# The prompt joins the projections' first pass over the sample, raw tokens are split, and the norm's root is multiplied in at the evacuations

## The chip, the cores and the metric

The kernel runs on one core of a Trainium2 chip. The metric is the device time of one execution in microseconds (us), as the median of several runs. The engines are PE (TensorE: matmuls; PEld its weight loads), DVE (VectorE), ACT (ScalarE), POOL (GpSimd) and SP (SyncE, which issues nearly all transfers). Each works through its own queue in order, and they wait for one another at semaphores.

## What is computed

One encoder layer is applied to a prompt of 256 tokens and a sample of 2048 tokens, with the same weights. The part that matters here is the first:

```python
h = rms_norm(x, norm_mix_g)
proj = h @ w_in
q, k, v, x_br, y_br = jnp.split(proj, splits, axis=-1)
q = rms_norm(q.reshape(B, S, N_Q_HEADS, HEAD_DIM), q_norm_g)
k = rms_norm(k.reshape(B, S, N_KV_HEADS, HEAD_DIM), k_norm_g)
...
attn = bidir_gqa(apply_axial_rope(q, tables), apply_axial_rope(k, tables), v)
rec = recurrent_group(x_br, y_br, conv_w, conv_b, lru_wa, lru_ba, lru_wx, lru_bx, lru_lambda)
x = x + jnp.concatenate([attn, rec], axis=-1) @ w_out
```

`rms_norm` divides a token by the root of its mean square, so the root is one number per token and could be taken before or after `h @ w_in`. `w_in` has 1024 rows and 1792 columns. The recurrent group runs a convolution, two gates and a forward and a backward scan on `x_br`, and multiplies by the gelu of `y_br`. After this come the output projection, an MLP and a last norm.

## The kernel before

All arrays lie feature-major (128 features on the partitions, tokens along the row). Every large matmul is done as three: weights and activations are each split into a rounded high part and a low remainder, and `mm3` adds high x high, high x low and low x high. `w_in` is cut into 14 blocks `m` of 128 output columns: 0 to 3 are the queries, 4 the keys, 5 the values, 6 to 9 the four recurrent channels, 10 to 13 the gelu's. `project` multiplies one block with one tile of tokens: 24 matmuls, 256 tokens wide for the prompt and 512 for each of the four sample tiles. Its sum stands in one of three PSUM banks (`m0` to `m2`, two while the prompt's attention holds `m2`), and `evac` moves it to SBUF.

The first stage makes three passes over the 14 blocks. The prompt's pass (`order_p`) loads each weight tile, rounds it (line 168), subtracts (line 177) and stores both parts; two passes over the sample follow, `ORDER_S` for tiles 0 and 1 and `ORDER_T` for tiles 2 and 3, which read the stored parts back. `WStream.advance` keeps these streams some tiles ahead.

`norm1` squares a tile of tokens, sums over features (a matmul with ones), takes the reciprocal root with a Newton step and multiplies the tokens by it; `norm1_split` then makes the parts `hh` and `hl` with the norm's gain. The pool of these parts holds two sets, so tiles 2 and 3 enter when the last block of tiles 0 and 1 has been multiplied.

Around the projections run generators, advanced by `tick` twice in each `project`: `do_gelu`, `do_qk` (head norm and rotary embedding), `do_v`, `lru` for one recurrent channel at a time, and `attention_p`, the prompt's attention for a pair of head blocks, started at block 1 of each sample pass and waited for before block 9 of the first and block 12 of the second. A scheduler with a timeline of its own sets the final order on each engine; `evac` has a raised priority. When the 28 sample block pairs are done, the second stage begins: the prompt's output projection and MLP, the backward scans (`lru_back`) and the sample's attention, interleaved, and then the four MLPs of the sample.

## Time and profile before

| | |
|---|---|
| median of 3 runs | 3201.34 us (3199.52 to 3202.33) |
| the profiled execution | 3204.86 us |
| its span, first to last instruction | 3203.1 us |
| busy share of the span: PE, DVE, ACT, POOL | 94%, 57%, 54%, 45% |
| mean granted TensorE clock | 0.966 of full speed |

Busy shares are means over stages that differ: PE is busy nearly throughout the long MLP and attention stages, and much less in the first quarter of the span. A matmul counts as busy from its start to a modelled end, and matmuls overlap, so the step from one start to the next is the better measure of what one costs.

### The profile page before, as it was taken

How to read it: one execution, taken by the hardware profiler on the slowest of the kernel's cores; microseconds unless marked ns; L12 is line 12 of the kernel's file. 1: busy time of each engine (PE TensorE's matmuls, PEld its weight loads, DVE VectorE, ACT ScalarE, POOL GpSimd, SP SyncE). 2: the span in 40 equal slices, each digit the busy share in tenths (PEclk: the TensorE clock that was granted, in tenths of full speed). 3: DMA queues.
4: the chain of work that ended last, by engine and by line, in shares of the span. 5: the costliest groups of instructions: out<-in, count | busy, mean ns of one | idle time of the engine just before them, and what ended most of it. 6: DMA issues, size and time to landing. Idle time of an engine off the chain costs nothing.

```text
span 3203.1 us, 41975 instructions
## 1 busy us (share of the span) xinstructions
PE 3009.3 (94%) x13646; PEld 2431.3 (76%) x13646; DVE 1823.7 (57%) x2602; ACT 1720.3 (54%) x2988; POOL 1438.2 (45%) x1117
## 2 busy tenths in 40 slices
PE   6699899678999899999999999999999999899998
PEld 5577677566888588888887888888878888778887
DVE  8878776699787754555556555555573311121114
ACT  5465666455666566555556655555566333343333
POOL 4436633577888654334356434433654201411104
PEclk7799999788999899999999999999999999999999
DMA  7656455888766554444456544444664655766554
GB/s 255 200 177 225 158 182 187 257 270 248 236 219 208 170 190 130 148 137 130 148 170 226 166 141 137 139 142 134 218 208 154 189 189 188 261 230 188 188 189 148
DMA packets 346044, 598.98 MB, mean 187 GB/s; under 512 B 44128, under 2 KB 77152, under 8 KB 345824
## 3 DMA queue, kind: packets, MB, share of 16 engines
q1 hardware_dynamic: 345824, 596.30, 58.0%
q8 instruction: 107, 1.75, 0.2%
q14 instruction: 113, 0.93, 0.1%
HBM read 474.52 MB, written 121.63 MB: 186 GB/s over the span
## 4 chain that ended last, share of the span: by engine, by line
PE 68%; DVE 7%; DMA 5%; ACT 3%; issue 2%; POOL 1%; SPq 1%; DVEq 0%; ACTq 0%; POOLq 0%
PE ps_d L204 8%; PE ps_d L202 8%; PE ps_d L203 8%; PE ps_u L204 8%; PE ps_u L203 8%; PE ps_u L202 8%; PE s_t L974 3%; PE s_t L975 3%; PE pq L980 3%; PE po L979 3%; PE s_mx L870 3%; PE ps_o L203 1%; PE ps_o L202 1%; PE ps_o L204 1%; DVE mx L871 1%
## 5 line engine op out<-in xcount | busy, mean ns | idle before, releaser
L990 POOL TENSOR_TENSOR acc<-acc,ph 128x512 f32<-128x512 f32 x448 | 598.8, 1337 | 534.1 <-ACT ph L984 521.6
L168 ACT CAST wh<-wf 128x512 fp32r<-128x512 f32 x712 | 440.2, 619 | 720.7 <-PE ps_d L203 296.2
L986 DVE TENSOR_TENSOR pl<-s_t,ph 128x512 fp32r<-128x512 f32 x512 | 349.6, 684 | 278.6 <-ACT ph L984 274.6
L204 PE MATMUL ps_u<-h2h,wl 128*128 128x512 f32 (+1 forms) x1280 | 479.4, 375 | 7.2 <-DMA wl<-wl_d 3.7
L202 PE MATMUL ps_u<-h2h,wh 128*128 128x512 f32 (+1 forms) x1280 | 478.4, 374 | 0.8 <-DVE xr L1013 0.8
L203 PE MATMUL ps_u<-h2l,wh 128*128 128x512 f32 (+1 forms) x1280 | 478.9, 374 | 0.0
L982 ACT ACTIVATE s_t<-s_t 128x512 f32<-128x512 f32 x512 | 298.1, 583 | 327.5 <-PE s_t L975 310.7
L202 PE MATMUL ps_d<-uh,wh 128*128 128x512 f32 (+1 forms) x1248 | 466.1, 373 | 2.1 <-ACT rl L1031 0.8
L204 PE MATMUL ps_d<-uh,wl 128*128 128x512 f32 (+1 forms) x1248 | 465.8, 373 | 2.2 <-DVE wl L177 1.3
L203 PE MATMUL ps_d<-ul,wh 128*128 128x512 f32 (+1 forms) x1248 | 465.3, 373 | 0.3 <-DVE ul L1035 0.2
L871 DVE TENSOR_REDUCE mx<-s_mx 128x1 f32<-128x512 f32 x512 | 344.1, 683 | 210.5 <-PE s_mx L870 208.8
L1033 POOL TENSOR_TENSOR rl<-rl 128x512 f32<-128x512 f32 (+1 forms) x160 | 159.2, 995 | 626.9 <-ACT uh L1032 620.5
L1146 DVE TENSOR_TENSOR y<-y,ps_d 128x512 f32<-128x512 f32 (+1 forms) x272 | 170.5, 627 | 323.3 <-PE ps_d L204 321.0
L984 ACT ACTIVATE ph<-s_t 128x512 fp32r<-128x512 f32 x512 | 304.7, 597 | 27.7 <-POOL acc L990 2.0
L1035 DVE TENSOR_TENSOR ul<-rl,uh 128x512 fp32r<-128x512 f32 (+1 forms) x160 | 145.9, 912 | 289.3 <-POOL rl L1033 289.2
L204 PEld LDWEIGHTS ps_u<-h2h,wl 128*128 128x128 f32 x1280 | 243.4, 190 | 57.4 <-DMA wl<-wl_d 5.0
L202 PEld LDWEIGHTS ps_u<-h2h,wh 128*128 128x128 f32 x1280 | 243.4, 190 | 50.9 <-DVE xr L1013 1.4
L203 PEld LDWEIGHTS ps_u<-h2l,wh 128*128 128x128 f32 x1280 | 243.3, 190 | 48.3 <-issue 0.5
L202 PEld LDWEIGHTS ps_d<-uh,wh 128*128 128x128 f32 x1248 | 236.4, 189 | 53.0 <-ACT rl L1031 2.2
L204 PEld LDWEIGHTS ps_d<-uh,wl 128*128 128x128 f32 x1248 | 236.1, 189 | 50.1 <-DVE wl L177 2.3
L203 PEld LDWEIGHTS ps_d<-ul,wh 128*128 128x128 f32 x1248 | 236.3, 189 | 48.0 <-DVE ul L1035 1.2
L202 PE MATMUL ps_in<-hh,wh 128*128 128x512 f32 (+1 forms) x560 | 220.8, 396 | 44.1 <-DVE wh L168 16.4
(281 smaller groups left out, 5704.2 us busy)
## 6 DMA issues: line engine op xcount, KB each, us to landing
wl<-wl_d SPq DMA_DIRECT2D x624, 256.0 KB, 2.7
wf<-in_w_up_dram SPq DMA_DIRECT2D x320, 256.0 KB, 3.0
wf<-in_w_down_dram SPq DMA_DIRECT2D x320, 256.0 KB, 3.0
wl_d<-wl SPq DMA_DIRECT2D x172, 256.0 KB, 3.0
wf<-in_w_out_dram SPq DMA_DIRECT2D x80, 256.0 KB, 4.0
wh<-wh_d SPq DMA_DIRECT2D x56, 256.0 KB, 3.4
x<-in_xT_dram SPq DMA_DIRECT2D x32, 256.0 KB, 4.8
qd<-q_ds SPq DMA_DIRECT2D x64, 128.0 KB, 3.0
```

Source lines behind the costliest of these rows:

```text
L168: self.copy(i)(tile_, self.f[i])
L202: mm(ps, wh, xh, start=first, stop=False)
L203: mm(ps, wh, xl, start=False, stop=False)
L204: mm(ps, wl, xh, start=False, stop=last)
L871: nc.vector.tensor_reduce(mx[:, i, b:b + 1], s[:, :w], axis=AX.X, op=ALU.max)
L982: act(s, s, AF.Exp)
L984: act(ph, s, AF.Copy)
L986: tt(pl, s, f32(ph), op=ALU.subtract)
L990: gtt(acc, acc, f32(ph), op=ALU.add)
L1033: gtt(e[:, :n], e[:, :n], e[:, :n], op=ALU.mult)
L1035: tt(ul[:, f, :n], e[:, :n], f32(uh[:, f, :n]), op=ALU.subtract)
L1146: tt(y[:, :n], y[:, :n], ps[:, :n], op=ALU.add)
```

## The change

There is no prompt pass any more. In the pass over tiles 0 and 1, each weight block is multiplied first with the prompt's 256 tokens, then with the two sample tiles; weights are loaded, split and stored in this pass and read back once, in the pass over tiles 2 and 3. The tokens are split into parts without the norm's root (`split`); the sum of squares and the root are made beside it (`squares`, `roots`), and `evac` multiplies by the root on DVE, where ACT copied before. The rounding of the weights goes to ACT after the first six tiles. In `do_gelu` a multiply leaves POOL and a scale-and-add leaves DVE for one DVE operation; in `do_qk` a square moves from POOL to ACT and a multiply from DVE to POOL. The split gate weights of a channel are stored at first use and read back later, where they were rebuilt each time. The prompt's attention runs wholly in the second pass. Both orders of blocks are new.

```diff
-NORM_AT = 9
+RAW_AT = 13
-ORDER_S = [6, 0, 2, 7, 13, 12, 8, 4, 1, 3, 11, 5, 9, 10]
-ORDER_T = [4, 5, 0, 6, 1, 10, 8, 2, 11, 7, 3, 12, 9, 13]
+ORDER_S = [0, 6, 1, 10, 7, 2, 11, 8, 3, 12, 9, 13, 4, 5]
+ORDER_T = [6, 4, 5, 7, 0, 1, 8, 2, 3, 9, 10, 11, 12, 13]
-PA_AT = [1, 1]
+PA_AT = 2
 PA_END = 12
...
-    def evac(dst, src):
+    def evac(dst, src, r):
+
         with tc.high_priority(offset=EVAC):
-            act(dst, src, AF.Copy)
+            tt(dst, src, r, op=ALU.mult)
...
-    ws = WStream(wp, srcs, saved, AHEAD, WBUFS, lambda i: nc.vector.tensor_copy if i < n1 else nc.scalar.copy,
+    ws = WStream(wp, srcs, saved, AHEAD, WBUFS, lambda i: nc.vector.tensor_copy if i < 6 else nc.scalar.copy,
...
+        g_d = [[dtile([P, 512], f"g{t}_d{c}") for t in "hl"] for c in range(4)]
+        gate_split = set()
+
 
         def load_gates(c):
+            if c in gate_split:
+                parts = [cp.tile([P, 2, 2, P], FR, tag=t, name=t, bufs=2) for t in ("wgh", "wgl")]
+                for t, d in zip(parts, g_d[c]):
+                    loadr(t.rearrange("p g d n -> p (g d n)"), d)
+                return parts
+            gate_split.add(c)
...
+            for t, d in zip((wgh, wgl), g_d[c]):
+                store(d, f32(t).rearrange("p g d n -> p (g d n)"))
...
-        def do_gelu(dst, n, ps):
+        def do_gelu(dst, n, ps, r):
             y = sl.tile([P, NT], F32, tag="gy", name="gy", bufs=2)
             z = sl.tile([P, NT], F32, tag="gz", name="gz", bufs=2)
-            evac(y[:, :n], ps[:, :n])
-            act(z[:, :n], y[:, :n], AF.Square)
-            ts(z[:, :n], z[:, :n], 0.044715, 1.0, op0=ALU.mult, op1=ALU.add)
-            yield
-            gtt(z[:, :n], z[:, :n], y[:, :n], op=ALU.mult)
+            evac(y[:, :n], ps[:, :n], r)
+            act(z[:, :n], y[:, :n], AF.Square, scale=math.sqrt(0.044715))
+            yield
+            stt(out=z[:, :n], in0=z[:, :n], scalar=1.0, in1=y[:, :n], op0=ALU.add, op1=ALU.mult)
             yield
...
-                gtt(t[:, :w], rr, rr, op=ALU.mult)
+                act(t[:, :w], rr, AF.Square)
...
-                tt(qq, qq, rr, op=ALU.mult)
+                gtt(qq, qq, rr, op=ALU.mult)
...
+        def enter(xs, t):
+
+            while not sets:
+                yield
+            sets.pop(0)
+            h = h_tiles()
+            yield from split(xs, *h)
+            h_s.append(h)
+            acc = yield from squares(xs, NT)
+            r = r_tile()
+            yield from roots(acc, NT, r)
+            r_s.append(r)
...
         for hf in range(2):
+            tiles = [("s", 2 * hf, NT * 2 * hf), ("s", 2 * hf + 1, NT * (2 * hf + 1))]
+            if hf == 0:
+                tiles = [("p", None, 0)] + tiles
             for ii, m in enumerate((order_s, order_t)[hf]):
-                i = len(order_p) + hf * len(order_s) + ii
+                i = hf * len(order_s) + ii
+                end = ii == len(order_s) - 1
                 ws.advance(2 * i)
-                if hf == 0 and ii == NORM_AT:
-                    while pa in ticks.active:
+                if hf == 0 and ii == RAW_AT:
+                    while convs.get(0, 1) or any(g in ticks.active for g in qk_p):
                         tick()
-                    banks[0] = itertools.cycle(("m0", "m1", "m2"))
-                    nxt = [load_x(SEQ + NT * t, NT, tag) for t, tag in ((2, "xb"), (3, "xa"))]
-                    spawn(norms(nxt))
-                if ii == PA_AT[hf]:
+                    entering.append((load_x(SEQ + 2 * NT, NT, x_tiles("xb")), 2))
+                if hf == 1 and ii == PA_AT:
                     banks[0] = itertools.cycle(("m0", "m1"))
-                    pa = spawn(attention_p([2 * hf]))
-                if hf and ii == PA_END:
+                    pa = spawn(attention_p([0, 2]))
+                if hf == 1 and ii == PA_END:
                     while pa in ticks.active:
                         tick()
                     banks[0] = itertools.cycle(("m0", "m1", "m2"))
...
+                for r, t, t0 in tiles:
+                    if t is None:
+                        ps = project(i, h_p, SEQ)
+                        root = r_p
+                        if 6 <= m < 10:
+                            x = xp.tile([P, NT], F32, tag="xb", name="xb_p")
+                            xb_p.append(x)
+                            nc.vector.memset(x[:, 0:2], 0.0)
...
+                        if end:
+                            entering.append((load_x(SEQ + 3 * NT, NT, x_tiles("xa")), 3))
+                        continue
+                    while len(h_s) <= t:
                         tick()
-                    ps = project(i, h_s[2 * hf + t], NT)
-                    if ii == len(order_s) - 1:
+                    ps = project(i, h_s[t], NT)
+                    if end:
                         sets.append(t)
+                    while len(r_s) <= t:
+                        tick()
+                    root = r_s[t]
+                    o = NT * (t % 2)
                     if 6 <= m < 10:
-                        evac(xb[:, off + NT * t:off + NT * t + NT], ps)
+                        evac(xb[:, off + o:off + o + NT], ps, root)
                     elif m >= 10:
-                        spawn(do_gelu(gel_d["s"][m - 10, :, t0:t0 + NT], NT, ps))
+                        spawn(do_gelu(gel_d["s"][m - 10, :, t0:t0 + NT], NT, ps, root))
```

The new functions (`split` and `squares` yield now and then, so that other work comes between):

```python
def split(xs, hh, hl):

    for k in range(KC):
        act(hh[k], xs[k], AF.Identity, scale=vcol(V_GMIX + k))
        stt(out=hl[k], in0=xs[k], scalar=vcol(V_GMIX + k), in1=f32(hh[k]), op0=ALU.mult, op1=ALU.subtract)
        if k % 2:
            yield

def squares(xs, n):
    acc = sb.tile([P, NT], F32, tag="acc", name="acc")
    for k in range(KC):
        if k == 0:
            act(acc[:, :n], xs[k], AF.Square)
        else:
            s = sb.tile([P, NT], F32, tag="b", name="sq", bufs=3)
            act(s[:, :n], xs[k], AF.Square)
            gtt(acc[:, :n], acc[:, :n], s[:, :n], op=ALU.add)
        if k % 2:
            yield
    return acc

def roots(acc, n, r):
    ps = ps_a.tile([P, 2, NT], F32, tag="st", name="ps_n")
    mm(ps[:, 0, :n], ones_d, acc[:, :n], start=True, stop=True)
    yield
    w = sb.tile([P, NT], F32, tag="b", name="w1", bufs=3)
    rsqrt_newton(ps[:, 0, :n], r, w[:, :n], tt)
    ts(r, r, -0.5, None, op0=ALU.mult)
    yield
...
def start():
    yield from split(xs_p, *h_p)
    ws.advance(0)
    acc = yield from squares(xs_p, SEQ)
    h = h_tiles()
    yield from split(xs0, *h)
    h_s.append(h)
    yield from roots(acc, SEQ, r_p)
    h = h_tiles()
    yield from split(xs1, *h)
    h_s.append(h)
    for xs in (xs0, xs1):
        acc = yield from squares(xs, NT)
        r_s.append(r_tile())
        yield from roots(acc, NT, r_s[-1])
```

At the start of the program, on PE: before, the prompt's blocks follow one another (`hh` and `hl` are the prompt's parts, each `wh`/`wl` number a weight tile, 256 wide).

```order
L203 MATMUL ps_in<-hl,wh_507 128x256
L204 MATMUL ps_in<-hh,wl_516 128x256
L202 MATMUL ps_in<-hh,wh_507 128x256
L203 MATMUL ps_in<-hl,wh_507 128x256
L204 MATMUL ps_in<-hh,wl_516 128x256
L202 MATMUL ps_in<-hh,wh_564 128x256
L203 MATMUL ps_in<-hl,wh_564 128x256
L204 MATMUL ps_in<-hh,wl_570 128x256
```

After, at the same place (`hp` are the prompt's parts, `hh` and `hl` now a sample tile's, 512 wide):

```order
L205 MATMUL ps_in<-hp,wl_431 128x256
L203 MATMUL ps_in<-hp,wh_422 128x256
L204 MATMUL ps_in<-hp,wh_422 128x256
L205 MATMUL ps_in<-hp,wl_431 128x256
L204 MATMUL ps_in<-hl,wh_419 128x512
L205 MATMUL ps_in<-hh,wl_428 128x512
L203 MATMUL ps_in<-hh,wh_419 128x512
L204 MATMUL ps_in<-hl,wh_419 128x512
```

A weight tile, split once (`wh_419`), now serves three token tiles in a row where it served the prompt alone.

On DVE in the first part of the program: before, in the prompt's pass, the rounding (`CAST`) and the subtraction of weight tiles stand in nearly every row.

```order
L168 CAST wh_903<-wf_896 128x512
L177 TENSOR_TENSOR wl_909<-wf_896,wh_903 128x512
L411 TENSOR_TENSOR wgl<-wgf,wgh 128x512
L168 CAST wh_1008<-wf_898 128x512
L177 TENSOR_TENSOR wl_1014<-wf_898,wh_1008 128x512
L429 TENSOR_SCALAR gz<-gz 128x256
L403 MEMSET wgf 128x512
```

After, the evacuations (line 197) of the first two blocks, behind the root (`r_527` is that of sample tile 0, `r_559` of tile 1):

```order
L324 TENSOR_SCALAR r_527<-r_527 128x512
L197 TENSOR_TENSOR qk<-ps_in,r_527 128x512
L197 TENSOR_TENSOR xb<-ps_in,r_527 128x512
L529 SCALAR_TENSOR_TENSOR xc<-xb,vec,xc 128x512 x2
L210 TENSOR_TENSOR w_562<-r_559 128x512
L211 SCALAR_TENSOR_TENSOR w_562<-ps_n,w_562 128x512
L212 SCALAR_TENSOR_TENSOR r_559<-w_562,r_559 128x512
L324 TENSOR_SCALAR r_559<-r_559 128x512
L197 TENSOR_TENSOR qk<-ps_in,r_559 128x512
```

The evacuations came onto DVE, and the first of each tile stands behind that tile's root.

At the end of the first stage, on PE: before, the last channel's gate matmuls (`ps_g`) follow the first twelve matmuls of the prompt's output projection (`ps_o`), which follow the last projection.

```order
L204 MATMUL ps_o<-cat_4915,wl_5249 128x256
L202 MATMUL ps_o<-cat_4915,wh_5245 128x256
L203 MATMUL ps_o<-cat_4917,wh_5245 128x256
L204 MATMUL ps_o<-cat_4915,wl_5249 128x256
L202 MATMUL ps_g<-xh,wgh 128x342
L203 MATMUL ps_g<-xl,wgh 128x342
L204 MATMUL ps_g<-xh,wgl 128x342
```

After, the prompt's attention (`pdenp`, its last matmuls) stands just ahead of the last 24 matmuls of the projections, and no gate matmul stands behind them:

```order
L205 MATMUL ps_in<-hh,wl_4917 128x512
L689 MATMUL pdenp<-ahp,ones_312 128x512
L689 MATMUL pdenp<-alp,ones_312 128x512
L689 MATMUL pdenp<-ahp,ones_315 128x512
L689 MATMUL pdenp<-alp,ones_315 128x512
L203 MATMUL ps_in<-hh,wh_4818 128x512
```

The recurrent tail moved ahead of the last blocks, and the end of the prompt's attention moved behind most of them.

## Rows read from the trace of the kernel before

**Rows 1.** Busy time by stretch: window, length, PE, PEld, DVE, ACT, POOL, clock, DMA, GB/s.

```profile
0.00:127.00 127.00, 77.28 (x404) 68.19 (x404) 108.14 (x183) 59.46 (x118) 62.41 (x50) 0.74 0.69 231
127.00:353.00 226.00, 205.07 (x843) 157.38 (x844) 178.70 (x226) 138.09 (x209) 111.06 (x72) 0.97 0.61 201
353.00:579.00 226.00, 204.43 (x872) 161.52 (x872) 161.54 (x202) 146.72 (x220) 99.07 (x63) 0.95 0.51 170
579.00:640.00 61.00, 38.96 (x185) 31.36 (x184) 39.48 (x50) 30.46 (x50) 30.45 (x22) 0.75 0.98 297
640.00:800.00 160.00, 128.16 (x644) 103.36 (x643) 149.11 (x187) 88.63 (x175) 119.70 (x91) 0.86 0.86 260
```

**Rows 2.** Timeline of ACT: the last evacuation of each pass; start, length.

```profile
126.92 0.38 ACT L196 ACTIVATE v<-ps_in 128x256 f32<-128x256 f32 x1 [2.75 <-PE ps_in L204]
...
352.16 0.58 ACT L196 ACTIVATE gy<-ps_in 128x512 f32<-128x512 f32 x1
...
578.88 0.60 ACT L196 ACTIVATE gy<-ps_in 128x512 f32<-128x512 f32 x1
```

**Rows 3.** Timeline of PE: first and last of 46 projection matmuls in a row.

```profile
310.03 0.39 PE L204 MATMUL ps_in<-hh,wl 128*128 128x512 f32 x1
...
320.26 0.39 PE L204 MATMUL ps_in<-hh,wl 128*128 128x512 f32 x1
```

**Rows 4.** Waits of PE, 0 to 127 us: total, times, longest.

```profile
PE ps_in L202 <- DVE wh L168: 16.4, 5, 6.4
PE ps_in L204 <- DVE wl L177: 13.0, 10, 3.6
```

**Rows 5.** Groups of DVE by shape, 0 to 579 us: count, busy, mean ns, idle before.

```profile
L331 DVE SCALAR_TENSOR_TENSOR hl<-x,vec,hh 128x512 fp32r<-128x512 f32 x32 | 29.9, 977 | 6.7 <-ACT hh L330 6.7
...
L177 DVE TENSOR_TENSOR wl<-wf,wh 128x512 fp32r<-128x512 f32 x29 | 24.7, 853 | 1.2
...
L478 DVE TENSOR_TENSOR ql<-qk,qh 128x512 fp32r<-128x512 f32 x20 | 22.6, 1132 | 5.2 <-ACT qh L476 5.0
L168 DVE CAST wh<-wf 128x512 fp32r<-128x512 f32 x28 | 21.4, 766 | 4.3 <-DMA wf<-in_w_in_dram 4.2
...
L429 DVE TENSOR_SCALAR gz<-gz 128x512 f32<-128x512 f32 x15 | 17.5, 1165 | 2.3 <-ACT gz L428 2.3
L471 DVE TENSOR_TENSOR qk<-qk,rq 128x512 f32<-128x512 f32 x20 | 16.7, 852 | 0.7 <-POOL qk L464 0.5
...
L468 DVE SCALAR_TENSOR_TENSOR wq<-ps_q,wq 128x512 f32<-128x512 f32 x22 | 14.8, 682 | 5.6 <-POOL wq L467 5.6
...
L411 DVE TENSOR_TENSOR wgl<-wgf,wgh 128x512 fp32r<-128x512 f32 x12 | 13.7, 1145 | 4.1 <-ACT wgh L409 4.1
...
L435 DVE SCALAR_TENSOR_TENSOR gz<-gz,gy 128x512 f32<-128x512 f32 x15 | 12.0, 798 | 11.6 <-ACT gz L433 11.6
...
L669 DVE RECIPROCAL rcp<-pdenp 128x512 f32<-128x512 f32 x2 | 6.7, 3358 | 0.1
...
L662 DVE TENSOR_TENSOR alp<-pfp,ahp 128x512 fp32r<-128x512 f32 x4 | 5.6, 1407 | 3.2 <-ACT ahp L661 3.2
L649 DVE TENSOR_TENSOR plp<-pfp,php 128x512 fp32r<-128x512 f32 x8 | 5.5, 683 | 0.5 <-ACT php L647 0.5
L631 DVE TENSOR_REDUCE mxp<-s_mxp 128x2 f32<-128x512 f32 x8 | 5.5, 683 | 3.4 <-PE s_mxp L629 3.4
```

**Rows 6.** Groups of POOL by shape, 0 to 579 us, same columns.

```profile
L315 POOL TENSOR_TENSOR x<-x,r 128x512 f32<-128x512 f32 x32 | 49.9, 1592 | 5.6 <-DVE r L310 5.6
...
L431 POOL TENSOR_TENSOR gz<-gz,gy 128x512 f32<-128x512 f32 x15 | 24.0, 1598 | 18.5 <-DVE gz L429 18.5
```

**Rows 7.** Waits of PE, 127 to 579 us: the longest in total.

```profile
PE ps_in L202 <- ACT qk L196: 10.5, 2, 5.6
```

**Rows 8.** Timelines of PE and DVE: first sample-attention matmul, last forward scan.

```profile
598.48 1.19 PE L870 MATMUL s_mx<-k,qd 128*128 128x512 f32 x2 [5.64 <-DMA qd<-q_ds]
...
605.81 4.08 DVE L560 TENSOR_TENSOR_SCAN s<-af,cfw,s 128x1026 f32<-128x1026 f32 x1
```

More of the change, by code (lines that the diff above doesn't have):

```diff
@@ L565, in lru_prompt @@
             done = []
[L566 removed]
+            gate_w.clear()
+            yield from lru([(xb[c], SEQ * c, SEQ, c) for c in range(4)],
                            [(SEQ * c, SEQ, c, None) for c in range(4)], 4 * SEQ, done, 0)
@@ L731, in trunk, with enter_all @@
-        sets.append(0)
+        def enter(xs, t):
+            while not sets:
+                yield
+            sets.pop(0)
[6 more added lines that the diff above has]
+            r_s.append(r)
+        entering = []
+        def enter_all():
+            while len(h_s) < 4:
+                while not entering:
+                    yield
+                xs, t = entering.pop(0)
+                yield from enter(xs, t)
```

201 lines of the change are left out of this document (82 added, 119 removed).

## The prediction

> **What bounds the kernel now.** I read the busy times by stretch first [rows 1], cut where the last evacuation of each pass over the projections stands [rows 2]: the prompt's pass ends at 127 us, the first half of the sample at 353 us, the second at 579 us. The reader should compare PE with DVE in each line. In the prompt's pass PE is busy 77 of 127 us and DVE 108, or 85%. PE's granted clock there is 0.74, between its two levels of 1.2 and 2.4 GHz, against 0.97 in the next stretch. In each half of the sample PE is busy 205 of 226 us and DVE only 179 and 162. From 579 to 640 us nobody is full (PE 39 and DVE 39.5 of 61), and from 640 to 800 us DVE is busy 149 of 160, or 93%. Behind 800 us the change does nothing; whatever it is worth must come from the first 640 us.
>
> The step of a sample matmul is (320.26 - 310.03)/45 = 0.227 us [rows 3]. The prompt's 336 matmuls have half the columns, so I estimate half the step, 0.114 us, and 38 us in all. The prompt's pass takes 127 us for 38 us of matmuls, because weights are prepared for a matmul that uses them only briefly: PE's longest waits in it are for the rounding of the weights (16.4 us) and for their subtraction (13.0 us), both on DVE [rows 4]. So the prompt's pass is bound by DVE and the sample's passes mostly by PE, with DVE having room beside it. The change lays the first two stretches over each other.
>
> **The merged pass.** Its PE work is that of the first half, 205 us busy, and 38 us of the prompt: 243 us. Its DVE work starts from 108.1 + 178.7 = 286.8 us [rows 1]. The durations below are in [rows 5]; a form 256 wide is put at half of the form 512 wide.
>
> Leaving DVE: 22 of 28 roundings, 22 x 0.766 = 16.9 us; the gelu's scale-and-add, 8 wide and 4 narrow, 8 x 1.165 + 4 x 0.58 = 11.6; the multiply of queries and keys by their root, 10 for the sample and 2 for the prompt, 12 x 0.852 = 10.2; four of eight gate splits, 4 x 1.145 = 4.6; and half of the prompt's attention, which moves to the second half: one reciprocal 3.36, two subtractions `alp` 2.8, four `plp` 2.7 and four reductions 2.7, together 11.6. That is 54.9 us.
>
> Coming to DVE: the evacuations, 28 wide and 14 narrow. The nearest row for an operation that reads one PSUM and one SBUF operand is the Newton step `wq<-ps_q,wq` at 0.682 us: 28 x 0.682 + 14 x 0.34 = 23.9. The gelu's new operation, priced as its sister on line 435, 8 x 0.798 + 4 x 0.4 = 8.0. The 16 remainders `hl` of tiles 2 and 3 now stand ahead of this pass's last evacuation: 16 x 0.977 = 15.6. That is 47.5 us. The sum is 286.8 - 54.9 + 47.5 = 279.4 us.
>
> The price of the evacuation rests on that row. An operation with two SBUF operands costs more here: 0.852 for `qk<-qk,rq`, 1.132 for `ql<-qk,qh` [rows 5]. If the evacuation cost 1.132, the 28 wide ones would add 12.6 us and the merged pass would be 14 us longer.
> The Trainium skill ("SBUF — State Buffer", section "SBUF: two separate sides") says that a DVE operation with two SBUF inputs is locked out while a GpSimd operation that reads SBUF holds the shared port pair, and by that rule an evacuation, with one SBUF input, is not. The trace agrees, 0.682 against 0.852 and 1.132 us; by the rule the lower price holds, without it the 14 us would be due.
>
> POOL loses the 32 multiplies of tokens by the root, 50 us, and the gelu's multiply, 8 x 1.598 + 4 x 0.8 = 16 us [rows 6], of 62.4 + 111.1 = 173.5 us busy in the two stretches; what else moves onto it and off it nearly cancels (the multiply of queries comes, a square goes). If DVE's lengthened forms shrink with POOL's share, by 66/173.5 = 38% of what they lie above 0.682 us (32 `hl`, 20 `ql` and 29 `wl`: 9.4 + 9.0 + 5.0 = 23 us), DVE loses 9 us more. I take 270 us, with 256 (all 23) and 279 (none) as ends.
>
> 270 us exceeds PE's 243, so DVE bounds the merged pass. How full it gets is read from the two stretches that DVE bounds: 85% in the first, which waits for its first loads, and 93% from 640 to 800 us. I take 91%, nearer to the second, since here too several generators feed the engine: 270/0.91 = 297 us against 353, a gain of 56 us. The ends are 279/0.85 = 328 (gain 25) and 256/0.93 = 275 (gain 78).
>
> What costs nothing here: the second reading of the weights that falls away (28 tiles, two parts each) was prefetched three tiles ahead, and the rounding moved to ACT (139 of 226 us busy in the first half) lies beside DVE. Covered by DVE's own queue is the lateness of the roots at the start: they need seven additions on POOL for the prompt and seven for each of two tiles, up to 1.59 us each by the nearest row [rows 6], so the first sample evacuation comes some 40 us in, while three banks hold only the 13.6 us of the first prompt and sample tiles. DVE splits 24 token tiles meanwhile; with that cover gone PE's wait would cost up to 10 us, which the 85% end contains.
>
> **The second half.** Here DVE gets 28 evacuations (19.1 us), the gelu (6.4) and the other half of the attention (11.6), and loses scale-and-adds (9.3), multiplies (8.5), gate splits (4.6) and the 16 remainders (15.6): 161.5 - 0.9. Its share stays, so does PE's work but for that half of the attention. I leave it its 226 us and add 4, a third of those 11.6, for a chain that waits for itself at many points. Ends: 12 us, all of it, and -6, if entering tiles 2 and 3 earlier shortens the start.
>
> **The tail.** Before, the last channel's block is the last but one of the pass: its forward scan ends at 605.81 + 4.08 = 609.9 us, 31 us behind the last evacuation, and the sample's attention begins at 598.48 [rows 2, 8]. In the new order four gelu blocks stand behind the last channel, so that chain lies under some 44 us of projections. DVE idles 21.5 us in that stretch [rows 1], and no more than that can come back. Against it the prompt's attention now ends last: behind its last matmuls come a reciprocal of 3.36 us, a multiply, a rounding, a store and a load before the prompt's output projection, and only 24 matmuls (5.5 us) cover them. I take 14 us of gain, with 0 and 21.5 as ends.
>
> **The sum.** The profiled execution took 3204.9 us, 3.5 over the median of 3201.3. 3204.9 - 56 + 4 - 14 = 3138.9; less 3.5 this is 3135. All ends together give 3201 - 105 = 3096 and 3201 - 13 = 3188.
>
> **The rivals.**
> DVE fills no better than in the prompt's pass (85%, gain 25), and the prompt's attention eats the tail: 3201 - 25 + 4 = 3180. For it speaks that loads, splits and roots all come at the start; against it that these are a fifth of the pass.
> DVE is not the bound. If contention goes and PE sets the pace at the 91% of the first half, the merged pass takes 243/0.91 = 267 us, a gain of 86, in all 3201 - 96 = 3105. Against it speaks that 270 us of DVE work do not fit into 267.
> The other side: the evacuations wait on DVE. While the prompt's attention runs, blocks 2 to 11 of the second half have two banks, 20 projections. The old evacuation on ACT cost PE 10.5 us in all [rows 7]. DVE's queue holds forward scans, one of 4.08 us [rows 8]; if each of the 20 projections waited once for so much, this would be 82 us, and the time 3135 + 82 = 3217. It decides from 66/20 = 3.3 us each. Against it: four forward scans in that half, one for each channel, not 20, and the raised priority.
> The Trainium skill ("TensorEngine Tiling (Array Packing)", section "PSUM Bottleneck") advises to use ScalarE and VectorE both for PSUM evacuation; all of them on one engine is what this rival would punish, and no row shows it yet.
> The change doesn't do what it says: waits for roots at the start and for tiles 2 and 3 at the half eat all but what a measurement tells, 0.2% or 6.4 us: 3195 to 3208.
>
> **The chances.** The forecast 0.55, the half-filled DVE 0.20, PE as the bound 0.10, late evacuations 0.09, no effect 0.06. So faster 0.85, the same 0.06, slower 0.09. The range 3098 to 3184 holds the first three and leaves out the rest.
>
> **What would show it.** Right: the merged pass's last evacuation at 275 to 328 us with DVE over 85% busy; evacuations at 0.63 to 0.72 us; PE's waits for weights on DVE gone; a clock over 0.9 behind the first 60 us; the last projection near 527 us and the sample's attention within 15 us of it. Wrong: DVE far under 85% with PE waiting for evacuations or for roots; the second half over 240 us; or a stall of over 15 us behind the prompt's attention at the end.

## The result and the profile after

The changed kernel takes 3169.46 us, median of 4 runs (3166.53 to 3173.47), the kernel before 3200.43 on the same chip (3194.66 to 3202.33). The ratio is 0.9907, with a 95% interval of 0.9888 to 0.9926: 31 us, or 0.9%, faster. The forecast was 66 us. The sign held, and the time lies in the range, but more than half of the gain is missing.

The busy times by stretch, cut behind the start (62 us), at the 41st of the merged pass's 42 evacuations (286), behind the first evacuations of tiles 2 and 3 (360) and at the last evacuation of the second half (561):

```profile
core 0: us, PE busy (x) PEld busy (x) DVE busy (x) ACT busy (x) POOL busy (x), PEclk, DMA share, GB/s
0.00:62.00 62.00, 38.72 (x152) 29.42 (x152) 47.33 (x104) 31.43 (x57) 27.14 (x27) 0.89 0.54 181
62.00:286.00 224.00, 204.88 (x1006) 169.41 (x1005) 174.60 (x245) 135.42 (x204) 70.90 (x42) 0.97 0.59 202
286.00:360.00 74.00, 47.20 (x165) 33.19 (x166) 55.89 (x79) 52.06 (x83) 40.06 (x26) 0.78 0.48 156
360.00:561.00 201.00, 179.72 (x793) 143.96 (x791) 156.79 (x195) 127.00 (x186) 76.78 (x47) 0.96 0.52 171
561.00:640.00 79.00, 52.56 (x226) 38.50 (x227) 49.14 (x69) 32.24 (x60) 40.44 (x31) 0.74 1.02 297
640.00:800.00 160.00, 129.28 (x732) 108.47 (x731) 137.06 (x186) 87.57 (x173) 117.72 (x92) 0.90 0.84 269
```

From 62 to 286 us PE is busy 91% and DVE 78%: it is PE that bounds the merged pass, as the experiment d2 confirms below. Then comes a hole: from 286 to 360 us PE issues 165 matmuls in 74 us at a granted clock of 0.78. In the stretch that follows it issues 793 in 201.

The evacuations on DVE's timeline: the last two of the merged pass, the first ones of tiles 2 and 3, and the end of the second half.

```profile
285.56 0.68 DVE L197 TENSOR_TENSOR v<-ps_in,r 128x512 f32<-128x512 f32 x1
...
318.01 0.69 DVE L197 TENSOR_TENSOR v<-ps_in,r 128x512 f32<-128x512 f32 x1 [0.91 <-PE pt L511]
...
339.73 0.69 DVE L197 TENSOR_TENSOR xb<-ps_in,r 128x512 f32<-128x512 f32 x1
...
355.84 0.69 DVE L197 TENSOR_TENSOR xb<-ps_in,r 128x512 f32<-128x512 f32 x1
...
535.78 0.69 DVE L197 TENSOR_TENSOR gy<-ps_in,r 128x512 f32<-128x512 f32 x1 [0.40 <-PE ps_in L205]
...
549.03 3.36 DVE L691 RECIPROCAL rcp<-pdenp 128x512 f32<-128x512 f32 x1
...
560.50 1.29 DVE L197 TENSOR_TENSOR gy<-ps_in,r 128x512 f32<-128x512 f32 x2 [1.63 <-PE ps_in L205]
```

The last evacuation of the first sample pass stands at 318.0 us instead of 352.2, and that of the second half at 561.1 instead of 578.9 [rows 2]. Between 535.8 and 560.5 us there is none; in that gap lies the reciprocal that ends the prompt's second attention pair. On PE's side (total, times, longest, 0 to 561 us):

```profile
PE ps_in L203 <- DVE xb L197: 15.0, 2, 14.0
PE ps_in L203 <- DVE lt L398: 13.4, 1, 13.4
PE ps_in L203 <- DVE qk L197: 9.7, 4, 4.0
PE ps_in L203 <- DVE rcp L691: 8.9, 1, 8.9
PE ps_in L205 <- DVE wl L177: 8.8, 6, 4.0
PE ps_in L204 <- DVE hl L301: 5.8, 5, 2.1
PE ps_in L203 <- ACT wh L168: 5.7, 3, 3.4
```

The waits for the weights, 16.4 and 13.0 us in the prompt's pass alone [rows 4], are 5.7 and 8.8 now. New are 14.0 us at 340 us, behind the evacuation that waits for tile 2's root, and 8.9 us behind the reciprocal. The 13.4 us are the time to the first matmul.

The sum in the prediction's terms, in the profiled executions (span 3203.1 before, 3164.8 after): the two passes over the projections end 17.8 us earlier, where 52 was forecast, and from the last evacuation to the end it is 2603.7 us instead of 2624.2, a gain of 20.5 where 14 was forecast. The missing time is in the projections. By the prediction's own marks, the last evacuation of each pass, the merged pass gains 34.2 us (352.2 to 318.0) where 56 was forecast, and the second half takes 16.4 more (243.1 against 226.7) where 4 was forecast; the run n3 below shows that the first mark is a wait for a buffer and not the end of the pass's work.

### The profile page after: what moved, and what is told of

Its sections match the earlier page's. It is cut to its first block, busy times and chain, and to the rows that moved or that the text cites. A ratio compares the mean times of both kernels' runs of the same rounds, so it can differ in the third digit from the quotient of the medians.

```text
span 3164.8 us, 41808 instructions
## 1 busy us (share of the span) xinstructions
PE 2980.7 (94%) x13632; PEld 2411.6 (76%) x13632; DVE 1793.0 (57%) x2609; ACT 1710.6 (54%) x2956; POOL 1368.2 (43%) x1071
## 4 chain that ended last, share of the span: by engine, by line
PE 73%; DVE 7%; DMA 5%; ACT 3%; issue 2%; POOL 1%; SPq 0%; DVEq 0%; ACTq 0%; POOLq 0%
PE ps_d L205 8%; PE ps_d L203 8%; PE ps_d L204 8%; PE ps_u L205 8%; PE ps_u L203 8%; PE ps_u L204 8%; PE s_t L1016 3%; PE pq L1022 3%; PE s_t L1017 3%; PE po L1021 3%; PE s_mx L912 3%; PE ps_o L203 2%; PE ps_o L204 2%; PE ps_o L205 1%; DMA k<-k_ds 1%
## 5 line engine op out<-in xcount | busy, mean ns | idle before, releaser
L168 ACT CAST wh<-wf 128x512 fp32r<-128x512 f32 x734 | 453.8, 619 | 751.6 <-PE ps_d L204 298.5
L1028 DVE TENSOR_TENSOR pl<-s_t,ph 128x512 fp32r<-128x512 f32 x512 | 350.1, 686 | 287.0 <-ACT ph L1026 283.4
L912 PE MATMUL s_mx<-k,qd 128*128 128x512 f32 x512 | 209.5, 419 | 27.1 <-DVE mx L913 12.6
```

The costliest lines, as they stand in the source:

```text
L168: self.copy(i)(tile_, self.f[i])
L912: mm(s[:, :w], qd[:, i * P:(i + 1) * P], k1[:, kv, b * w:(b + 1) * w], start=True, stop=True)
L1028: tt(pl, s, f32(ph), op=ALU.subtract)
```

## The experiments

Times are medians; the three columns on the right come from one profiled execution of each run. The column "41st" is the start of the 41st evacuation (values of tile 0, the last but one of the merged pass), "last" that of the last evacuation of the second half, "rest" the span less that, and the "half" is the pass over tiles 2 and 3. The kernel before, measured beside each group on its chip, took 3199 to 3203 us.

| run | us | ratio to before, 95% interval | 41st | last | rest |
|---|---|---|---|---|---|
| changed kernel | 3169.5 | 0.9907 [0.9888, 0.9926] | 285.6 | 561.1 | 2603.7 |
| r0 (the same again) | 3171.4 | 0.9912 [0.9897, 0.9927] | 287.3 | 561.8 | 2606.4 |
| n1 roots of the second half | 3178.7 | 0.9941 [0.9925, 0.9958] | 285.9 | 572.1 | 2604.5 |
| p5 squares first | 3178.9 | 0.9933 [0.9920, 0.9947] | 287.6 | 567.5 | 2606.6 |
| n3 buffer of the values | 3183.5 | 0.9952 [0.9936, 0.9967] | 286.0 | 565.0 | 2616.7 |
| n2 roots of the first pass | 3157.9 | 0.9874 [0.9855, 0.9893] | 276.0 | 550.5 | 2602.9 |
| d2 first pass evacuated on ACT | 3158.5 | 0.9861 [0.9847, 0.9876] | 285.0 | 560.2 | 2599.3 |
| d1 second half on ACT | 3179.8 | 0.9922 [0.9909, 0.9935] | 292.6 | 567.7 | 2613.1 |
| d3 rounding on DVE | 3179.2 | 0.9924 [0.9911, 0.9937] | 295.6 | 568.4 | 2610.3 |
| t1 late last channel | 3173.1 | 0.9915 [0.9902, 0.9929] | 287.0 | 552.7 | 2619.1 |
| a1 one attention pair | 3157.7 | 0.9866 [0.9849, 0.9883] | 286.8 | 545.8 | 2603.6 |
| a2 more banks | 3164.7 | 0.9888 [0.9873, 0.9903] | 288.6 | 545.7 | 2622.0 |
| o1 spread queries | 3174.7 | 0.9912 [0.9900, 0.9924] | 285.9 | 554.5 | 2616.7 |
| x3 attention first | 3177.5 | 0.9932 [0.9914, 0.9950] | 287.1 | 548.2 | 2632.4 |
| a3 = a1 + n1 | 3170.3 | 0.9908 [0.9893, 0.9923] | 286.9 | 550.3 | 2619.4 |
| x5 = a1 + o1 | 3152.3 | 0.9841 [0.9821, 0.9860] | 287.5 | 541.5 | 2611.6 |
| x4 = x3 + o1 | 3154.2 | 0.9859 [0.9842, 0.9875] | 286.5 | 543.9 | 2608.8 |
| x2 = a1 + n1 + o1 | 3142.6 | 0.9826 [0.9807, 0.9846] | 288.0 | 534.6 | 2605.9 |
| f1 = x4 + start on PE | 3155.9 | 0.9858 [0.9841, 0.9875] | 277.5 | 537.1 | 2613.3 |

n1, n2, d1, d2, a1, a3, x5 and x2 leave out some of the work or use wrong roots, as told at each; the others compute what the changed kernel does. Roots and spread without the pair were not run together.

Two things must be read from the columns first. None of these edits touches a line that computes behind the projections, yet the rest takes anything from 2599 to 2632 us. Some edits move the end of a channel or of the prompt's attention across the line between the columns, but n3, which only changes one buffer ahead of it, has 13 us more in the rest as well; how that comes is not shown. So a difference of some 10 us in the total says little about the edit; what an edit does to the projections is read from the two columns of evacuations, and the total is named where it agrees. The columns have a spread too: in the runs whose edits act only behind the 41st evacuation, it stands at 285.6 to 288.6 us, and in d1 at 292.6.

### The half boundary: is it the roots?

**n1** makes the roots of tiles 2 and 3 but lets nobody wait for them; it multiplies by those of tiles 0 and 1 instead:

```diff
-            r = r_tile()
-            yield from roots(acc, NT, r)
-            r_s.append(r)
+            yield from roots(acc, NT, acc)
...
-                    root = r_s[t]
+                    root = r_s[t % 2]
```

> Leaves out the right roots of the sample's second half: its evacuations multiply by the first half's roots, which are long there; the squares, sums and roots of tiles 2 and 3 are still made, into the tile of their sums, and nobody waits for them. Theory (late roots stall the half boundary): the wait of 14.0 us at 340 goes, the first evacuations of tiles 2 and 3 come at about 323 and 338 us instead of 339.7 and 355.8, and the run takes 12 to 18 us less than the changed kernel's 3169. Rival (DVE's queue is full there whatever the roots do): the first evacuations move by under 4 us and the time by under 6.

The first evacuation of the half came at 304.4 us instead of 339.7, and PE issued 240 instead of 165 matmuls from 286 to 360 us. But the last evacuation came 11 us later, and the total is 7 to 9 us more. Windows of n1, and PE's waits in it from 360 to 572 us:

```profile
286.00:360.00 74.00, 61.82 (x240) 47.86 (x241) 53.42 (x84) 45.19 (x74) 37.03 (x26) 0.89 0.54 179
360.00:561.00 201.00, 160.85 (x694) 127.49 (x692) 153.40 (x186) 128.06 (x190) 76.41 (x46) 0.90 0.47 158
```

```profile
PE ps_in L203 <- DVE qk L197: 12.1, 2, 7.8
PE s_mxp L651 <- DVE mxp L653: 11.8, 2, 8.4
PE pdenp L689 <- DVE osbp L681: 6.8, 2, 6.6
```

The lead of 75 matmuls is given back: 694 against 793 in the next stretch. The new waits are for evacuations of queries and for steps of the prompt's attention. Both theories failed: the wait for the roots is real, and taking it away alone gains nothing.

**p5** makes the squares of tiles 2 and 3 ahead of the wait for a free set, and the roots behind four of the eight remainders.

```diff
+            acc = yield from squares(xs, NT)
             while not sets:
                 yield
...
-            yield from split(xs, *h)
-            h_s.append(h)
-            acc = yield from squares(xs, NT)
+            parts = split(xs, *h)
+            for _ in range(2):
+                next(parts)
+                yield
             r = r_tile()
             yield from roots(acc, NT, r)
             r_s.append(r)
+            yield from parts
+            h_s.append(h)
```

> Computes the same as the changed kernel. For tiles 2 and 3 the squares and their sums are made before the wait for a free set of split tokens, and the roots behind the first four of the eight remainders. Theory (late roots): the first evacuations of tiles 2 and 3 at 305 to 315 and 320 to 335 us instead of 339.7 and 355.8, and 15 to 28 us less than 3169. Rival (DVE's queue or PE's order sets that stretch): under 6 us.

The first evacuation of tile 2 came at 339.1 us, as late as ever, and the total is 7 to 9 us more. POOL began to add the squares at 295.0 us instead of 309.5, but the last of its seven additions ended at 322.8, against 325.3 in the changed kernel: between them stand the queries' multiplies and the channel's remainders. DVE, which makes the root from that sum, was busy 61.7 of the 74 us from 286 on, against 55.9. So more than the order of the squares makes the roots late.

**n3** gives the values of tile 1 another buffer:

```diff
-            v = sl.tile([P, NT], F32, tag="gy", name="v", bufs=2)
+            v = sl.tile([P, NT], F32, tag="gz" if r == "s" and t0 == NT else "gy", name="v", bufs=2)
```

> The evacuated values of tile 1 get a buffer of the tag gz instead of the third use of two buffers of the tag gy. Theory: the last evacuation of the merged pass comes at 292 to 300 us instead of 318.0, but the next evacuations still wait for the roots until about 338 us, so the time changes by under 6 us. Rival (the bank held by that evacuation was what delayed the second half): 10 to 16 us less than 3169.

Its last evacuation of the merged pass, and the first of tile 2:

```profile
294.71 0.68 DVE L197 TENSOR_TENSOR v<-ps_in,r 128x512 f32<-128x512 f32 x1
...
344.50 0.69 DVE L197 TENSOR_TENSOR xb<-ps_in,r 128x512 f32<-128x512 f32 x1
```

So the merged pass is over at 294.7 us; the 318.0 of the changed kernel is a wait for a buffer (its row above names the transposes `pt` that free it). The half gains nothing from it: the next evacuation is 5 us later than before the edit. Of the 12 to 14 us more in the total, 3 to 4 lie in the projections and the others in the rest.

### What bounds the merged pass

**n2** multiplies the first pass by a constant column, so nobody waits for its roots.

```diff
-                        root = r_p
+                        root = one.to_broadcast([P, SEQ])
...
-                    root = r_s[t]
+                    root = r_s[t] if hf else one.to_broadcast([P, NT])
```

> Leaves out the roots of the first pass: its evacuations multiply by a constant of one column, laid out by a zero step; all roots are still made. Theory of the prediction (the start is covered by the splitting of tokens on DVE): the first evacuation comes earlier than 34.4 us, but the 41st, at 285.6 us, moves by under 5 us. Rival (the start is lost time, since PE sets the pace behind it): the 41st comes 12 to 20 us earlier, and the run takes 8 to 20 us less than 3169.

The 41st evacuation came 9.6 us earlier and the last one 10.6: what the start loses is not covered, but carried to the end. That is the rival, a little smaller than the 12 to 20 us expected; the total, 3157.9, agrees with it.

**d2** moves the evacuations of the first pass to ACT, and **d1** those of the second half (the first two lines, in the one pass alone). Both scale by the first column of the root, so they wait for it but leave out the right values. **d3** gives the rounding back to DVE.

```diff
-            tt(dst, src, r, op=ALU.mult)
+            act(dst, src, AF.Identity, scale=r[:, 0:1])
...
-    ws = WStream(wp, srcs, saved, AHEAD, WBUFS, lambda i: nc.vector.tensor_copy if i < 6 else nc.scalar.copy,
+    ws = WStream(wp, srcs, saved, AHEAD, WBUFS, lambda i: nc.vector.tensor_copy if i < n1 else nc.scalar.copy,
```

> Leaves out the right roots of the first pass: its 42 evacuations run on ACT, scaled by the first column of the root. The prediction's claim (DVE bounds the merged pass): 24 us leave DVE and the 41st evacuation, at 285.6 us, comes 15 to 25 us earlier. Rival (PE sets the pace there, 91% busy from 62 to 286 us against DVE's 78%): it moves by under 6 us.

> Leaves out the right roots of the second half: its 28 evacuations run on ACT, scaled by the first column of the root, so that they still wait for it. Theory (DVE's queue paces the second half, whatever wait shows first): 28 x 0.68 = 19 us leave DVE, the last evacuation comes at 545 to 553 us instead of 561.1, and the run takes 8 to 18 us less than the changed kernel's 3169. Rival (the half's chains, not DVE's load): within 5 us, or slower since ACT now evacuates late.

> Computes the same. The rounding of the projections' weights goes back from ACT to DVE for all 28 tiles of the first pass, as in the kernel before. The prediction's claim (DVE bounds the merged pass): 22 roundings of 0.41 to 0.77 us, 9 to 17 us, come back, and the 41st evacuation moves from 285.6 to 295 to 304 us. Rival (PE sets the pace): it moves by under 4 us, and the run by under 6.

Windows of d2:

```profile
62.00:286.00 224.00, 206.61 (x1006) 171.23 (x1004) 153.72 (x208) 154.78 (x239) 69.83 (x42) 0.95 0.59 201
286.00:360.00 74.00, 47.67 (x166) 33.08 (x167) 56.46 (x80) 54.41 (x88) 41.53 (x26) 0.80 0.47 159
```

DVE loses 21 us of 175 from 62 to 286 us, and PE issues the same 1006 matmuls: DVE's load does not bound the merged pass. That d2's total is 11 us lower can't come from there, since its last evacuation stands where it did. In d1 the 41st evacuation moved by 7 us, ahead of the edited half and for no reason that these runs show, but from it to the last it is 275.1 us, as in the changed kernel (275.5): 19 us less on DVE bought nothing there either. d3 is another matter. The 41st moved by 10 us. The work up to it, first in the changed kernel, then in d3:

```profile
0.00:285.60 285.60, 243.60 (x1157) 198.83 (x1157) 221.54 (x348) 166.45 (x260) 98.05 (x69) 0.96 0.58 197
0.00:295.60 295.60, 245.97 (x1151) 201.05 (x1152) 230.37 (x372) 156.82 (x240) 97.30 (x69) 0.92 0.56 190
```

DVE does 8.8 us more and is busy 78% of the time in both. PE's waits from 62 to 296 us in d3 show where the time goes:

```profile
PE ps_in L203 <- DVE wh L168: 18.2, 4, 7.0
```

Weights that are rounded in DVE's queue come late, though DVE is idle 22% of the time. The expectation's number came true; its reason, a full DVE, does not fit d2, where 25 us less of DVE's work moved nothing. Whether the added work or the place in the queue delays the weights was not tried apart.

### What paces the second half

**a1** leaves out the second pair of the prompt's attention:

```diff
-                    pa = spawn(attention_p([0, 2]))
+                    pa = spawn(attention_p([0]))
...
+                    for jj in (j, j + 2):
+                        store(a_d["p"][jj:jj + 2, i].rearrange("j p n -> p j n"), f32(t).rearrange("p (j n) -> p j n", j=2))
```

> Leaves out the second pair of the prompt's attention (its two head pairs 2 and 3): the first pair's result is stored in both places. Theory (the prompt's attention, now both pairs in the second half and all of it through the one bank m2, is a chain about as long as the half, and it, not the roots, sets where the half ends): the gap of 25 us ahead of the last two evacuations closes, the last stands at 530 to 542 us instead of 561.1, and the run takes 18 to 28 us less than the changed kernel's 3169. Rival (the half is bound by what PE and DVE have to do in it): only the pair's own work goes, some 6 us of each, and 5 to 10 us less.

The last evacuation came 15.3 us earlier, and the total is 12 to 14 us less; the theory's ends were 18 and 28, the rival's 5 and 10. So the pair's chain (a sequence of steps that each wait for the one before) has a part in where the half ends, but does not set its whole length. How long it is the reciprocals show, each the end of a pair, first the kernel before, then the changed one:

```profile
L669 DVE RECIPROCAL rcp<-pdenp x2: 3358/3358/3358, 262.7 to 476.2; 128x512 f32<-128x512 f32 x2
```

```profile
L691 DVE RECIPROCAL rcp<-pdenp x2: 3348/3352/3357, 433.3 to 549.0; 128x512 f32<-128x512 f32 x2
```

Before, a pair ended in each half, at 266 and 480 us, and the second half went on for 100 us behind it. From its first maximum (171.9 and 382.2 us) to that end a pair took 94 and 97 us. Now both follow each other through one bank, from 348.5 (the first maximum) to 552.4 us.

**a2** takes two of six steps of a round off that bank (the cut shows one of the two), **t1** puts the last channel where it was, **o1** puts other blocks between those of the queries.

```diff
...
-                            s = ps_m.tile([P, NT], F32, tag="m2", name="s_tp")
+                            if c:
+                                s = ps_g.tile([P, NT], F32, tag="g", name="s_tp")
+                            else:
+                                s = ps_m.tile([P, NT], F32, tag="m2", name="s_tp")
...
-ORDER_T = [6, 4, 5, 7, 0, 1, 8, 2, 3, 9, 10, 11, 12, 13]
+ORDER_T = [6, 4, 5, 7, 0, 1, 8, 2, 3, 10, 11, 12, 9, 13]
...
-ORDER_T = [6, 4, 5, 7, 0, 1, 8, 2, 3, 9, 10, 11, 12, 13]
+ORDER_T = [6, 4, 5, 7, 0, 10, 1, 8, 2, 11, 3, 9, 12, 13]
```

> Computes the same. The second score tile of each maximum and the second of each exponent come from the three banks of the gates instead of m2, so that four instead of six steps of each of the four rounds share the bank. Theory (one bank makes the chain long): pair 2 ends 20 to 45 us earlier, the last evacuation at 535 to 550 us, 8 to 22 us less than 3169. Rival (the chain's length is PE's order between steps, or the gates then wait for banks): within 6 us or slower.

> Computes the same. In the order of the second half the last channel's block stands last but one, as in the kernel before; the gelu blocks move up. Theory (the early last channel is the tail's gain, since its scans then lie under projections): first backward scan of the sample at 600 to 625 us instead of 585.8, and 14 to 24 us more than 3169. Rival (the end of the prompt's attention hides it): within 6 us.

> Computes the same. The order of the second half spreads the blocks of queries: 6, 4, 5, 7, 0, 10, 1, 8, 2, 11, 3, 9, 12, 13, so two gelu blocks stand between them and two behind the last channel. Theory (the queries' chain on two buffers is one of those that pace the half): the waits behind query evacuations in the second half go, 4 to 12 us less than 3169. Rival (the prompt's attention and the channels' chain pace it): within 5 us, or slower since less lies behind the last channel.

a2 ended the chain at 521.7 us instead of 552.4, and the projections 15 us earlier, as its theory had it. But the last channel's forward scan began at 575.6 instead of 544.3 us, the rest took 18 us more, and the total is only 5 to 7 us less, as its rival had it. The gates share their banks with the attention in a2; that this is what delayed the channel is not shown.

In t1 the projections end 8 us earlier, and the rest is 2619.1 us, 15 more than 2603.7, so that the total can't be told from the changed kernel's, as the rival had it. The sample's first backward scan came at 591.3 us, not at the 600 to 625 of the theory; counted from the last evacuation that is 38.6 us instead of 24.7. This agrees with some 14 us for the early last channel, but the rest varies by as much without such an edit, so the price rests on the place of that scan.

In o1 the projections end 7 us earlier, but PE then stands still from 546.9 to 562.5 us, until the prompt's attention is loaded for the first `ps_o`: one chain is shortened, and the next shows. The total is 3 to 5 us more, which is its rival.

**x3** gives the attention's steps the priority that evacuations have, and **x4** adds o1's order to it.

```diff
+        def first(g):
+            while True:
+                with tc.high_priority(offset=EVAC):
+                    if next(g, g) is g:
+                        return
+                yield
...
-                    pa = spawn(attention_p([0, 2]))
+                    pa = spawn(first(attention_p([0, 2])))
```

**a3**, **x5** and **x2** put the edits of a1, n1 and o1 together as the table says; **r0** is the base beside them.

> Computes the same. The prompt's attention gets the priority that evacuations have, so that its steps stand some two projections earlier in the engines' orders. Theory (its chain ends the half): the gap ahead of the last two evacuations shrinks from 25 us to under 15 and the run takes 6 to 14 us less than the changed kernel. Rival (what it takes from the other chains comes back as other waits): within 5 us.

> Computes the same. The priority of x3 and the spread query blocks. Theory (both chains shortened): 10 to 20 us less than the changed kernel, and more than x3 alone. Rival: the same as x3 within 4 us.

> Both omissions: one pair of the prompt's attention, and the second half's evacuations take the first half's roots. Theory (with the chain gone the late roots are what is left): 10 to 16 us less than the run with one pair alone. Rival (roots don't matter at all): the same as that run within 5 us.

> Leaves out the second pair of the prompt's attention and spreads the query blocks; the roots are as in the changed kernel. If the late roots are one of three parallel chains: 8 to 16 us more than the run with all three removals, 3151 to 3159. If they don't matter: within 4 us of its 3143, and the last evacuation within 6 us of 534.6.

> Leaves out the second pair of the prompt's attention and the right roots of the second half, and spreads the query blocks (6, 4, 5, 7, 0, 10, 1, 8, 2, 11, 3, 9, 12, 13). Theory (three chains of nearly the same length end the half together): the last evacuation at 515 to 530 us instead of 561.1 and 25 to 40 us less than the changed kernel, though the single removals gave +9, +5 and -12. Rival (the half is paced by something else): no less than the one pair alone, 3150 to 3160.

> The changed kernel itself, as the base for the three runs beside it: 3164 to 3174 us.

Read by the last evacuation (561.8 in r0): roots alone +10, spread alone -7, pair alone -16; roots and pair -12, spread and pair -20, all three -27. Counted from the 41st the steps are the same within 2 us. The edit that costs 10 us by itself gains 7 more once the other two are gone (541.5 to 534.6). In x5, with the late roots left, PE's longest wait from 286 to 545 us is again the one for tile 2's first evacuation, 12.8 us; in x2 none is longer than 4.7 us.

```profile
PE ps_in L203 <- DVE xb L197: 16.8, 2, 12.8
```

That is what chains of nearly equal length look like. The totals follow it, 3152.3 and 3142.6, though the intervals of these two ratios overlap, so that last step rests on the trace. x2's last evacuation, 534.6, is 4.6 us behind what the theory gave. a3's total is 13 us above a1's, which neither of its expectations had; its last evacuation is 4.5 us later and its rest 16 us longer.

x3 shortened the projections by 13.6 us and lost more than that in the rest, 2632.4, so that its total is 6 us above r0's. x4, which computes all that the changed kernel does, takes 3154.2 us, 17 less than r0 beside it, with intervals that do not meet, as its theory had it. Its two attention pairs took 180 us, from 346.3 to 525.9, instead of 204. PE's longest waits in it from 360 to 545 us:

```profile
PE ps_in L203 <- DVE xb L197: 3.4, 2, 1.9
PE ps_in L203 <- DVE qk L197: 2.9, 1, 2.9
```

**f1** adds to x4 a start in which PE sums the squares:

```diff
+            for k in range(KC):
+                s = sb.tile([P, NT], F32, tag="b", name="sq", bufs=3)
+                act(s[:, :n], xs[k], AF.Square)
+                mm(ps[:, 0, :n], ones_d, s[:, :n], start=k == 0, stop=k == KC - 1)
```

> Computes the same. The attention's priority and the spread query blocks, and at the start the eight squares of the prompt and of tiles 0 and 1 are summed by PE into the bank instead of by POOL. Theory (the start is lost time because PE sets the pace behind it): the first evacuation at 18 to 26 us instead of 34.4, the 41st 6 to 11 us earlier, and the run 6 to 11 us less than 3154. Rival (DVE's splits set the start): within 4 us of 3154.

Its first and its 41st evacuation:

```profile
21.05 0.42 DVE L197 TENSOR_TENSOR q_p<-ps_in,rp 128x256 f32<-128x256 f32 x1
...
277.47 0.68 DVE L197 TENSOR_TENSOR v<-ps_in,r 128x512 f32<-128x512 f32 x1
```

Against x4, the projections follow the theory (9.0 us earlier at the 41st, 6.8 at the last); the total, which is the same as x4's, follows the rival. The rest took 4.5 us more, and the profiled span is 2.3 us shorter; why the median isn't stays open.

## Why the prediction was right and where it was wrong

**The second half: the step that failed.** "I leave it its 226 us and add 4, a third of those 11.6, for a chain that waits for itself": +4, with ends of -6 and 12. From its forecast start at 297 us the half would have ended at 527. It ended at 561.1, so the term is +38 when counted from 297 us, and still +16 when the half is counted from the last evacuation at 318.0 to the end (243.1 us against 226.7). Three things in it were costed as work, or not at all, and are chains: the attention pair that moved in was priced at 11.6 us of DVE, but the two pairs take 204 us one behind the other; the query blocks come too close for their two buffers (spread, the half ends 7 us earlier); and the evacuations that wait for the roots of tiles 2 and 3 come 45 and 61 us behind the end of the merged pass, 294.7 us. They end nearly together, so no single removal gains its own length; all three together gave 27 of the 34 us between 561.1 and 527, with the second pair's own work among them, which x2 leaves out. x4, which leaves out nothing, got back 18. The other 7 us are not explained.

**The merged pass: the size came out, the mechanism didn't.** The forecast was 297 us, because "270 us exceeds PE's 243, so DVE bounds the merged pass". PE bounds it, at 91% from 62 us on, which was the second rival's mechanism; with the evacuations on ACT (d2) the 41st did not move. Of the two sums PE's held: it is busy 243.6 us up to the 41st and 251 up to 295 us. DVE's was too large: it is busy 221.5 us up to there and 250 up to 318.7, not 270. The rival's 267 us were too early in part because the start loses what the prediction called "covered by DVE's own queue": without the wait for the first roots the 41st is 9.6 us earlier (n2), and 9.0 in f1. The prediction had said that without this cover the wait "would cost up to 10 us". The work of the pass ends at 294.7 us (n3), two from the forecast. With DVE's sum too large and the bound the wrong one, that nearness is luck. The 23 us from there to the last evacuation at 318.0 are a buffer's.

**The price of an evacuation** held: 0.66 to 0.69 us for the wide form on DVE, 0.41 to 0.43 for the narrow one, where 0.682 and 0.34 were taken. Beside it an operation with two SBUF operands on the same tile (minimum, median and maximum in ns):

```profile
L197 DVE TENSOR_TENSOR qk<-ps_in,r x20: 656/682/693, 48.4 to 471.1; 128x512 f32<-128x512 f32 x20
...
L500 DVE TENSOR_TENSOR ql<-qk,qh x20: 675/692/2489, 82.0 to 511.1; 128x512 fp32r<-128x512 f32 x20
```

Of 20 evacuations none is stretched, of the 20 others some are, to 2489 ns. By the rule of the Trainium skill ("SBUF — State Buffer", section "SBUF: two separate sides"), of these two forms only the one with two SBUF inputs is locked out while a GpSimd operation that reads SBUF holds the shared port pair; the two rows agree.

**The rival of late evacuations** did not come about by DVE's load: d1 and d2 take it off DVE, and the projections do not end sooner. The Trainium skill ("TensorEngine Tiling (Array Packing)", section "PSUM Bottleneck") advises, where tiling has sped up TensorE, to use ScalarE and VectorE both for PSUM's evacuation; these runs show no gain in the passes from the other engine, and sharing the evacuations between both wasn't run.

**The last rival** had waits for roots, at the start and for tiles 2 and 3, eat nearly all of the gain. Both waits are there, 9.6 us at the start and 14.0 at the half, but they ate only a part of it, and taking the second away alone gained nothing (n1).

**The tail** gave 20.5 us where 14 was forecast, with 21.5 as the end; as the rest varies with edits ahead of it, the 6.5 us between them say little. t1 has 15.4 us more in the rest without the early last channel, near the 14, but this order costs 8 us ahead of it, which the prediction didn't count.

**The signs.** Of those for a right forecast, three came: the price of the evacuation, the merged pass's last evacuation between 275 and 328 us (318.0), and the sample's attention within 15 us (its first matmul at 572.9 us, 11.8 behind the last evacuation); DVE over 85% (78%), the weights' waits gone (14.5 us left), a clock over 0.9 behind the start (0.78 from 286 to 360 us) and the last projection near 527 us did not. Three that it named for a failure were there: PE waiting for a root with DVE under 85%, "the second half over 240 us" (243.1) and "a stall of over 15 us behind the prompt's attention at the end" (24.7 without an evacuation, from 535.8 to 560.5).

**The sum.** -52 became -17.8 and -14 became -20.5: 27.7 us short in the profiled executions. The median differs by 34.5 us from the forecast, since the profiled execution after took 2.9 us less than its median, where 3.5 us more was carried over from before.

What stays open: why the rest varies by 33 us with edits ahead of it, and by that a part of every total here.

## What to carry to other kernels

When a change moves a latency-bound sequence beside another one of its kind, price it by the time it took from first to last step, not by the engine time of its operations: the trace of before had it, 94 and 97 us for the two pairs, with 100 us of cover behind the second. Where several such chains end together, an experiment that removes one can show less than its length, or a loss; remove them together, and then put them back one at a time. And read an edit at the place where it acts before reading it in the total, when what stands behind varies with edits that don't touch it.

## What the runs showed of the hardware

DVE's operations on two SBUF operands got shorter without any edit to them. Groups of DVE by shape, 0 to 561 us (count, busy, mean ns, idle before), against [rows 5]:

```profile
L301 DVE SCALAR_TENSOR_TENSOR hl<-x,vec,hh 128x512 fp32r<-128x512 f32 x32 | 24.6, 801 | 0.0
...
L177 DVE TENSOR_TENSOR wl<-wf,wh 128x512 fp32r<-128x512 f32 x29 | 22.2, 765 | 8.1 <-ACT wh L168 7.9
...
L500 DVE TENSOR_TENSOR ql<-qk,qh 128x512 fp32r<-128x512 f32 x20 | 19.6, 983 | 12.1 <-ACT qh L498 7.5 <-POOL qk L488 2.4 <-DMA k_ds<-ql 1.8
```

They lost 5.3, 2.5 and 3.0 us, 10.8 together, where the prediction had 9 for POOL's smaller share; that POOL is the cause wasn't tried apart. And a hole costs more than its own length. From 286 to 360 us PE stands still once for 14.0 us and several times for 2 to 4, and its granted clock is 0.78; in the kernel before it was 1.00 in the same window. Behind the 14.0 us the clock is at the lower of its two levels, 1.2 GHz, for 4.8 us, and wide matmuls of the projections start every 0.43 us instead of every 0.23, some 2 us more for these 11 matmuls. The kernel before, then the changed one behind the hole:

```profile
286.00:360.00 74.00, 67.12 (x283) 51.05 (x281) 59.52 (x79) 38.15 (x64) 50.03 (x34) 1.00 0.61 205
340.50:345.30 4.80, 4.80 (x11) 3.77 (x12) 4.41 (x7) 2.58 (x7) 3.03 (x3) 0.50 0.39 153
```
